# Relative bias loaded as ready rows, and the order of the first loop's loads

## The chip, the cores and the metric

The kernel runs on one core of one Trainium2 chip. Its time is device microseconds of one execution; a lower time is better. Before the change the median of three runs is 983.15 us (982.04 to 983.37).

## The reference, cut to what matters

One decoder block works on 256 tokens of width 1024. A conditioning vector c gives, by one large matrix product, six modulation vectors (shift, scale and gate for the attention half and for the expert half). Then:

```
mod = (silu(c) @ ada_w + ada_b).reshape(6, D_MODEL)
h   = rmsnorm(x, norm1_g) * (1 + sc_a) + sh_a
x   = x + g_a * mixer(h)        # mixer: proj = h @ w_in (1024 x 2840), then attention, then w_out
h   = rmsnorm(x, norm2_g) * (1 + sc_f) + sh_f
x   = x + g_f * peer_ffn(h)     # 16384 experts, top 16 of them for each of 8 heads
out = rmsnorm(x, final_g)
```

The mixer has eight heads of sparse attention in three branches and four heads of differential attention. To the logits of all twelve heads a relative bias is added, `rel_bias[t5_bucket(t - s), head]`: it depends on the distance of query t and key s alone, through 32 buckets. Keys behind the query are masked.

## The kernel before, in words

All tensors lie with 128 partitions. The matrix products of the first half are done in three passes of fp32r: each operand x is split into hi (a cast on ScalarE) and lo (x minus hi, on VectorE), and a product is hi·hi + hi·lo + lo·hi (`mm3`, lines 88 to 91, three matmuls).

The projection loop (lines 246 to 284) goes over the eight slices of 128 rows of the model width, k = 0 to 7. One k-step needs four tiles of 512 KB from memory: two of weights (`w_inK` and `w_inK2`, tile `raw`, a pool of five) and two of modulation weights (`ada_w`, rows of the shift and of the scale, tile `adaw`, four of them). `k_load` (226) issues the four on SP's queue. `k_prep` (230) works on them: VectorE multiplies each modulation tile with the conditioning vector and sums (`ada_sum`, 150; the accumulated value is one column of `mod`); ScalarE casts both weight tiles (lines 73 and 237) and VectorE forms their lo parts (74 and 243); VectorE forms `gs` (239) and the normed slice `t` (241), from which ScalarE makes h_hi (242) and VectorE h_lo (244). `k_mm` (246) then issues 48 matmuls of 128x256 into all eight PSUM banks: 24 with the first weight tile, 24 with the second. The hi and lo parts of the first tile (`w_hi`, `w_lo`) have three buffers, those of the second (`wb`) two. Loads run two steps ahead, `k_prep` one step ahead of the matmuls.

Before the loop, c is loaded and brought to all partitions by two matmuls (262), x is squared and summed (266 to 269), and its root and reciprocal give `rstd1` (270, 271).

The bias comes into being on the chip. A one-hot matrix of the buckets over 384 distances and the table (`buckets`, loaded first on SP after c) are multiplied on TensorE (`bias_sum`, 182), giving one row of 384 values for each head. POOL's queue writes this row 32 times to memory (`fdr`, 180) and reads it back in four transfers of 32 partitions, each partition shifted by one element (`bias_load`, 187), so that `bias[p, head, m]` holds the bias of distance 128 + p - m, with the sign turned. In the program these two stand in step 6; POOL has nothing else to do before them.

From line 129 to 665 the order of instructions is written out by hand, engine by engine (`manual_schedule`). The rest (mixer, expert stage) is ordered by a planner from its own costs, for the mixer after the list `ORDER`; it may put an instruction from behind the loop between two of the loop's on an engine. `lambdas` (193) and the evacuation of the eight banks (661 to 664) close the part ordered by hand. Then come the mixer with its own weights (`w_inA`, `w_inB`, `cmp_w1`, in tiles of the same pool `raw`) and 24 further modulation tiles, from about 78 to 215 us, and the expert stage to the end.

Of the kernel before, what the change touches and what calls it, by code (L numbers as in the profile page):

```python
# [13 lines left out]
F32 = mybir.dt.float32  # L14
# [10 lines left out]
P = 128  # L25
# [17 lines left out]
T = 256  # L43
EPS = 1e-6
NEG = -1e30
# [12 lines left out]
def block_kernel(ctx: ExitStack, tc: tile.TileContext, I, out):  # L58
    nc = tc.nc
    V, S, G, PE = nc.vector, nc.scalar, nc.gpsimd, nc.tensor  # L60
# [4 lines left out]
    dram = ctx.enter_context(tc.tile_pool(name="dram", bufs=1, space=bass.MemoryType.DRAM))  # L65

    def load(src, n=D, pool=None, name="raw", **kw):
        t = (pool or raw_pool).tile([P, D], F32, name=name, **kw)
        nc.sync.dma_start(t[:, :n], src)
        return t  # L70
# [48 lines left out]
    early = early_stack.enter_context(tc.tile_pool(name="early", bufs=1))  # L119

    def bank(tag):
        return (pst if tag == "tr" else psp).tile([P, 512], F32, name=tag)
# [22 lines left out]
    def ada_load(ct):  # L145
        w = early.tile([P, D], F32, name="adaw", bufs=4)
        nc.sync.dma_start(w, I["ada_w"][ct])
        return w

    def ada_sum(ct, w):  # L150
        return V.tensor_tensor_reduce(out=w, in0=w, in1=cond, scale=D / 2, scalar=0.0,
                               op0=ALU.mult, op1=ALU.add, accum_out=mod[:, ct:ct + 1])
# [12 lines left out]
    V.memset(rowmask[0:31], 0.0)  # L165
    nlam = one.tile([P, 1], F32, name="nlam")
    subs = one.tile([P, 1], F32, name="subs")
    hflat = early.tile([P, 1348], F32, name="small")
    buckets = hflat[0:64, 0:396]
    fsb = hflat[0:12, 512:896]  # L170
    lam = hflat[:, 1024:1280].rearrange("p (a b) -> p a b", a=4)
    lj = hflat[:, 1280:1344]
    ls = hflat[:, 1344:1348]
    R = 32
    fdr = dram.tile([12, R, 384], F32, name="fdr")

    def late_loads():
        nc.sync.dma_start(cmpc, I["cmp_small"])
        nc.sync.dma_start(hflat[:, 1024:1280], I["lam"].partition_broadcast(P))
        nc.gpsimd.dma_start(fdr, fsb[:, None, :].to_broadcast([12, R, 384]))  # L180

    def bias_sum():
        fps = bank("tr")
        PE.matmul(fps[:12, :384], buckets[:, 384:396], buckets[:, 0:384], start=True, stop=True)
        S.copy(fsb, fps[:12, :384])

    def bias_load():
        for a in range(P // R):
            nc.gpsimd.dma_start(bias[a * R:(a + 1) * R],
                                bass.AP(tensor=fdr.tensor, offset=fdr.offset + 127 - a * R,  # L190
                                        ap=[[383, R], [384 * R, 12], [1, T]]))

    def lambdas():

# [29 lines left out]
    wts = {}  # L224

    def k_load(k):
        wts[k] = [load(I["w_inK"][k]), load(I["w_inK2"][k])]
        wts[k, "ada"] = [ada_load(k), ada_load(8 + k)]

    def k_prep(k):  # L230
        a, b = wts[k]
        for i in range(2):
            ada_sum(8 * i + k, wts[k, "ada"][i])
        wts[k][0] = split_tile(a)
        hl = [early.tile([P, D], F32R, name=f"wb{l}", bufs=2) for l in range(2)]
        wts[k][1] = hl
        S.copy(hl[0], b)
        V.tensor_add(mod[:, k:k + 9:8], mod[:, k:k + 9:8], ada_b[:, k:k + 9:8])
        V.scalar_tensor_tensor(gs[:, k:k + 1], mod[:, 8 + k:9 + k], 1.0, n1[:, k:k + 1], ALU.add, ALU.mult)
        t = early.tile([P, T], F32, name="nrm", bufs=2)  # L240
        V.scalar_tensor_tensor(t, xT[:, k], gs[:, k:k + 1], rstd1, ALU.mult, ALU.mult)
        S.activation(h1[0][:, k], t, AF.Identity, bias=mod[:, k:k + 1])
        V.tensor_sub(hl[1], b, hl[0].bitcast(F32))
        V.scalar_tensor_tensor(h1[1][:, k], t, mod[:, k:k + 1], h1[0][:, k].bitcast(F32), ALU.add, ALU.subtract)

    def k_mm(k):
        if not pre:
            pre.extend(bank(t) for t in ("mm", "mm", "tr", "tr", "lg", "lg", "o", "o"))
        for i in range(16):
            w, c = (wts[k][0], i * P) if i < 8 else (wts[k][1], (i - 8) * P)  # L250
            c = slice(c, c + P)
            mm3(pre[i // 2][:, (i % 2) * T:(i % 2 + 1) * T], (w[0][:, c], w[1][:, c]), (h1[0][:, k], h1[1][:, k]),
                k == 0 and i % 2 == 0, k == KD - 1 and i % 2 == 1)

    nc.sync.dma_start(buckets, I["buckets"])
    for i in range(2):
        nc.sync.dma_start(xT[:, 4 * i:4 * i + 4], I["x"][:, 4 * i:4 * i + 4])
    k_load(0)
# [6 lines left out]
    for k in (0, 4):  # L265
        S.activation(sq1[:, k:k + 4], xT[:, k:k + 4], AF.Square)
        V.tensor_add(sq1[:, k:k + 2], sq1[:, k:k + 2], sq1[:, k + 2:k + 4])
        V.tensor_add(sq1[:, k], sq1[:, k], sq1[:, k + 1])
        PE.matmul(ss[:, :T], rms_ones, sq1[:, k], start=k == 0, stop=k == 4)
    S.activation(rstd1, ss[:, :T], AF.Sqrt, bias=eps_t)  # L270
    V.reciprocal(rstd1, rstd1)
    bias_sum()
    k_load(1)
    k_prep(0)
    for k in range(KD):
        if k == 6:
            late_loads()
        if k + 2 < KD:
            k_load(k + 2)
        if k + 1 < KD:  # L280
            k_prep(k + 1)
        if k == 6:
            bias_load()
        k_mm(k)
    lambdas()
    early_stack.close()
    wk_stack = ph1.enter_context(ExitStack())
# [938 lines left out]
        outputs(False, None)  # L1226


def bucket_onehot():
    m = np.arange(384)  # L1230
    d = 255 - m
    n = np.maximum(d, 0)
    nf = np.maximum(n, 1).astype(np.float32)
    large = 16 + (np.log(nf / np.float32(16)) / np.float32(math.log(8.0)) * np.float32(16)).astype(np.int32)
    b = np.where(n < 16, n, np.minimum(large, 31))
    o = np.zeros((64, 384), np.float32)
    dd = d >= 0
    o[b[dd], m[dd]] = -1.0
    o[32, ~dd] = -1.0
    return o  # L1240


def layouts(a):
    c = np.ascontiguousarray
    o = {}
    o["x"] = c(a["x"].reshape(T, KD, P).transpose(2, 1, 0))
    o["c"] = c(a["c"].reshape(D))
    table = np.full((64, 12), np.float32(NEG))
    table[:32] = a["rel_bias"]
    o["buckets"] = c(np.concatenate([bucket_onehot(), table], axis=1))  # L1250
    o["ada_w"] = c(a["ada_w"][0].T.reshape(48, P, D))
    o["rows"] = c(np.concatenate([a["norm1_g"].reshape(KD, P).T, a["norm2_g"].reshape(KD, P).T,
                                  a["ada_b"].reshape(48, P).T, a["diff_subln_g"].reshape(P, 1)], axis=1))
    w = a["w_in"][0]
    def colsT(w, c0):
        return w[:, c0:c0 + P].reshape(KD, P, P).transpose(1, 0, 2).reshape(P, D)

    def colsK(cols, w=w):
        return np.concatenate([w[:, c0:c0 + P].reshape(KD, P, P) for c0 in cols], axis=2)

    wq = w.copy()
    wq[:, :512] = w[:, :512].reshape(D, 2, 4, 64).transpose(0, 2, 1, 3).reshape(D, 512)
    start = dict(k0=768, k1=1024, ck=512, cv=640)
    for i in range(4):
        start.update({f"q{i}": P * i, f"dq{i}": 1304 + P * i, f"dk{i}": 1816 + P * i})
    o["w_inK"] = c(colsK([start[n] for n in CHUNKS[:8]], wq))
    o["w_inK2"] = c(colsK([start[n] for n in CHUNKS[8:]], wq))
    wa = np.concatenate([w[:, 896:1024], w[:, 1152:1280], w[:, 1280:1304]], axis=1)
    o["w_inA"] = c(wa.reshape(KD, P, 280).transpose(1, 0, 2).reshape(P, KD * 280))
    o["w_inB"] = c(w[:, 2328:2840].reshape(KD, P, 512).transpose(1, 0, 2).reshape(P, KD * 512))  # L1270
    o["w_out"] = c(a["w_out"][0].reshape(2, 4, P, 4, 256).transpose(3, 0, 2, 1, 4).reshape(4, 2, P, D))
    pos = a["cmp_pos"][0]
    pos = np.concatenate([pos[:, :16].transpose(2, 0, 1), pos[:, 16:].transpose(2, 0, 1)], axis=0)
    w1 = a["cmp_w1"][0].reshape(2, 2, 4, 4, 64, 256)
    o["cmp_w1"] = c(w1.transpose(0, 2, 1, 4, 3, 5).reshape(2, 4, P, D))
    w2 = np.tile(a["cmp_w2"][0].reshape(2, 2, P, 64).transpose(2, 0, 1, 3), (1, 1, 1, 2))
    o["cmp_small"] = c(np.concatenate([pos.reshape(P, 32), w2.reshape(P, 512)], axis=1))
    o["lam"] = c(np.concatenate([a[n].reshape(64) for n in ("lam_q1", "lam_k1", "lam_q2", "lam_k2")]))
    o["peer_wq"] = c(np.stack([colsT(a["peer_wq"][0], i * P) for i in range(16)]))
    o["peer_sub_keys"] = c(a["peer_sub_keys"][0].transpose(2, 0, 1))  # L1280
    o["peer_u"] = c(a["peer_u"][0].reshape(P, P, KD, P).transpose(1, 3, 2, 0).reshape(P, P, D))
    o["peer_v"] = c(a["peer_v"][0].reshape(P, P, D).transpose(1, 0, 2))
    o["final_g"] = c(a["final_g"])
    return o
# [12 lines left out]
```

## Time and profile before

| | |
|---|---|
| profiled execution | 982.88 us |
| its span, first to last instruction | 980.8 us |
| median of three runs | 983.15 us |
| TensorE matmul, weight load busy | 934.2 us (95%), 686.2 us (70%) |
| VectorE, ScalarE, GpSimd busy | 766.8 us (78%), 494.2 us (50%), 17.9 us (2%) |
| read from memory | 193.22 MB |

Times of rows are counted from the span's start. PE is TensorE, PEld its weight loads, DVE VectorE, ACT ScalarE, POOL GpSimd, SP SyncE, which here only issues transfers; a q behind a name (SPq) is the engine's instruction queue. Matmuls overlap each other, so the distance of two starts is what one costs. The granted clock is a share of the full 2.4 GHz.

### The profile page before, as it was taken

To read this page: it belongs to the slowest core of one execution; us is meant where nothing else is said; L and a number is where in the kernel's file an instruction comes from. 1 tells how busy PE (TensorE), PEld (TensorE's weight loads), DVE (VectorE), ACT (ScalarE), POOL (GpSimd) and SP (SyncE) were. 2 spreads that over 40 slices of the span, in tenths; PEclk is the share of its full clock that TensorE was granted. 3 is DMA by queue.
4 is the path that set the end of the run, shared out by engine and by line. 5 is a ranking of instruction groups with operands and counts; after the bars stand their busy time and mean duration, and the time that the engine had idled before them with its cause. 6 is when DMAs were issued, how large, how long until landed. Compare 5 with 4: busy or idle time off the path is not lost.

```text
span 980.8 us, 18690 instructions
## 1 busy us (share of the span) xinstructions
PE 934.2 (95%) x7120; PEld 686.2 (70%) x7120; DVE 766.8 (78%) x2033; ACT 494.2 (50%) x899; POOL 17.9 (2%) x32
## 2 busy tenths in 40 slices
PE   5698997989999999999999999999999999999995
PEld 3697776979888888889999999544444443454442
DVE  6597879778657599658888888799999998656564
ACT  4246876475323365544444444544544554555542
POOL 0100010000000000000000000000000000000001
PEclk9899899899999999999999999999999999999998
DMA  8997646677554345765555555665555669756631
GB/s 285 319 329 252 218 130 211 224 252 263 174 193 151 108 166 179 248 203 177 190 175 191 175 187 179 204 205 193 184 189 188 214 208 332 235 178 207 199 124 48
DMA packets 54709, 198.26 MB, mean 202 GB/s; under 512 B 6269, under 2 KB 6605, under 8 KB 54226
## 3 DMA queue, kind: packets, MB, share of 16 engines
q1 hardware_dynamic: 52642, 189.90, 58.0%
q0 software_dynamic: 1248, 5.33, 2.1%
q10 hardware_dynamic: 720, 1.74, 0.5%
q8 instruction: 58, 0.95, 0.4%
q14 instruction: 41, 0.34, 0.1%
HBM read 193.22 MB, written 3.74 MB: 201 GB/s over the span
## 4 chain that ended last, share of the span: by engine, by line
PE 81%; DVE 7%; DMA 6%; ACT 3%; issue 2%; SPq 0%; DVEq 0%; ACTq 0%
PE y L1089 28%; PE up L89 11%; PE up L91 11%; PE up L90 11%; PE up L877 4%; PE gps L1000 3%; DMA raw<-in_ada_w_dram 3%; DMA adaw<-in_ada_w_dram 2%; PE mm L90 1%; PE mm L91 1%; PE mm L89 1%; PE lg L362 1%; PE o L536 1%; DVE w_lo L74 1%; PE gps L885 1%
## 5 line engine op out<-in xcount | busy, mean ns | idle before, releaser
L1089 PEld LDWEIGHTS <-wt 128*128 128x128 f16 x1500 | 143.9, 98 | 170.2 <-DVE wt L806 4.7
L805 ACT ACTIVATE w_lo<-raw 128x1024 f16<-128x1024 f32 x128 | 135.3, 1057 | 173.9 <-PE y L1089 83.3
L805 ACT ACTIVATE w_hi<-raw 128x1024 f16<-128x1024 f32 x128 | 135.2, 1056 | 170.5 <-PE up L91 85.4
L806 DVE SCALAR_TENSOR_TENSOR w_lo<-raw,w_lo 128x1024 f16<-128x1024 f32 x128 | 156.5, 1222 | 62.9 <-ACT w_lo L805 60.5
L806 DVE SCALAR_TENSOR_TENSOR w_hi<-raw,w_hi 128x1024 f16<-128x1024 f32 x128 | 156.2, 1220 | 54.6 <-ACT w_hi L805 54.4
L1089 PE MATMUL y<-w_hi,wt 128*128 128x512 f16 x756 | 174.0, 379 | 2.1 <-DVE wt L806 2.1
L1089 PE MATMUL y<-w_lo,wt 128*128 128x512 f16 x744 | 171.0, 379 | 0.2
L89 PE MATMUL up<-h,w_hi 128*128 128x256 f16 x512 | 139.6, 273 | 2.1 <-ACT bq L777 2.1
L90 PE MATMUL up<-h,w_hi 128*128 128x256 f16 x512 | 139.6, 273 | 0.0
L91 PE MATMUL up<-h,w_hi 128*128 128x256 f16 x512 | 139.6, 273 | 0.0
L89 PE MATMUL up<-h,w_lo 128*128 128x256 f16 x504 | 137.4, 273 | 0.0
L90 PE MATMUL up<-h,w_lo 128*128 128x256 f16 x504 | 137.4, 273 | 0.0
L91 PE MATMUL up<-h,w_lo 128*128 128x256 f16 x504 | 137.4, 273 | 0.0
L806 DVE SCALAR_TENSOR_TENSOR wt<-st,wt 128x256 f16<-128x256 f32 x128 | 53.7, 420 | 4.7 <-ACT wt L805 4.7
L90 PEld LDWEIGHTS <-w_hi 128*128 128x128 f16 x512 | 50.1, 98 | 8.2 <-issue 2.3
L805 ACT ACTIVATE wt<-st 128x256 f16<-128x256 f32 x128 | 51.3, 401 | 7.6 <-PE y L1089 5.6
L90 PEld LDWEIGHTS <-w_lo 128*128 128x128 f16 x512 | 50.1, 98 | 6.0
L91 PEld LDWEIGHTS <-w_lo 128*128 128x128 f16 x512 | 50.1, 98 | 5.8
L91 PEld LDWEIGHTS <-w_hi 128*128 128x128 f16 x512 | 50.1, 98 | 5.8
L89 PEld LDWEIGHTS <-w_lo 128*128 128x128 f16 x512 | 50.1, 98 | 5.7
L89 PEld LDWEIGHTS <-w_hi 128*128 128x128 f16 x512 | 50.2, 98 | 5.5
L984 DVE TENSOR_TENSOR B<-iota,kT 128x576 f16<-128x576 f16 (+1 forms) x64 | 27.2, 425 | 28.8 <-PE gps L1000 28.8
(370 smaller groups left out, 1505.8 us busy)
## 6 DMA issues: line engine op xcount, KB each, us to landing
raw<-in_peer_u_dram SPq DMA_DIRECT2D x128, 512.0 KB, 3.5
raw<-in_peer_v_dram SPq DMA_DIRECT2D x128, 512.0 KB, 4.2
adal<-in_ada_w_dram SPq DMA_DIRECT2D x24, 512.0 KB, 4.3
raw<-in_w_inK_dram SPq DMA_DIRECT2D x16, 512.0 KB, 8.3
adaw<-in_ada_w_dram SPq DMA_DIRECT2D x16, 512.0 KB, 8.6
wraw<-in_peer_wq_dram SPq DMA_DIRECT2D x12, 512.0 KB, 4.4
raw<-in_cmp_w_dram SPq DMA_DIRECT2D x8, 512.0 KB, 5.0
raw<-in_w_out_dram SPq DMA_DIRECT2D x8, 512.0 KB, 4.3
```

Source lines behind the costliest of these rows:

```text
L74: return (eng or V).tensor_sub(lo, src, hi.bitcast(F32))
L89: PE.matmul(ps, w[0], m[0], start=start, stop=False)
L90: PE.matmul(ps, w[0], m[1], start=False, stop=False)
L91: PE.matmul(ps, w[1], m[0], start=False, stop=stop)
L362: PE.matmul(out, q[x][pr, ts], rhs, start=i == 0, stop=i == 2)
L536: PE.matmul(o[:, h * 64:(h + 1) * 64], pt[:, h * P:(h + 1) * P], vst[sb][:, b, g], start=False, stop=bi == len(blocks) - 1 and h == 3)
L805: S.activation(hi, src, AF.Copy, scale=scale, **kw)
L806: V.scalar_tensor_tensor(lo, src, scale, hi, ALU.mult, ALU.subtract, accum_out=chk[:, i:i + 1])
L877: PE.matmul(ps, w[:, k * P:(k + 1) * P], h2[:, k], start=k == 0, stop=k == KD - 1)
L984: V.tensor_tensor(pairs(x), io, kT[:, i, t0:t0 + NT, None, :].to_broadcast(four), ALU.is_equal)
L1000: PE.matmul(ps[:, q, 0:n], A[:, q], Bg[i][:, q], start=i == 0, stop=i == 1)
L1089: PE.matmul(yps[t][n], w[:, ts], m[:, ns], start=j == 0 and first, stop=j == NJ - 1 and last)
```

## The change

- The host lays out the whole bias, 128 x 12 x 256 values, by indexing the table (`bias_rows`); the kernel loads it in one transfer on SP, in `late_loads`, which stands in step 6, behind the loads of step 7. The matrix of buckets, the matmul, the copy, the write to `fdr` and the four loads from it are gone, with 1024 of the 1348 columns of the tile `small`.
- The sign is turned on the chip: three multiplications by -1 on ScalarE behind the loop's last `k_mm`.
- `k_load` issues the two modulation tiles first, then the two weight tiles.
- `w_inK2` has three tiles of its own (`raw2`, in the pool that closes after the loop); `w_inK` keeps the pool `raw`.
- The modulation sums of step 0 stand ahead of the square root and the reciprocal of the norm.

```diff
-    hflat = early.tile([P, 1348], F32, name="small")
-    buckets = hflat[0:64, 0:396]
-    fsb = hflat[0:12, 512:896]
...
+    hflat = early.tile([P, 324], F32, name="small")
...
     def late_loads():
         nc.sync.dma_start(cmpc, I["cmp_small"])
-        nc.sync.dma_start(hflat[:, 1024:1280], I["lam"].partition_broadcast(P))
-        nc.gpsimd.dma_start(fdr, fsb[:, None, :].to_broadcast([12, R, 384]))
-
-    def bias_sum():
-        fps = bank("tr")
-        PE.matmul(fps[:12, :384], buckets[:, 384:396], buckets[:, 0:384], start=True, stop=True)
-        S.copy(fsb, fps[:12, :384])
-
-    def bias_load():
-        for a in range(P // R):
-            nc.gpsimd.dma_start(bias[a * R:(a + 1) * R],
-                                bass.AP(tensor=fdr.tensor, offset=fdr.offset + 127 - a * R,
-                                        ap=[[383, R], [384 * R, 12], [1, T]]))
+        nc.sync.dma_start(hflat[:, 0:256], I["lam"].partition_broadcast(P))
+        nc.sync.dma_start(bias, I["bias"])
...
     def k_load(k):
-        wts[k] = [load(I["w_inK"][k]), load(I["w_inK2"][k])]
         wts[k, "ada"] = [ada_load(k), ada_load(8 + k)]
+        wts[k] = [load(I["w_inK"][k]), load(I["w_inK2"][k], pool=early, name="raw2", bufs=3)]
+
+    def k_sums(k):
+        for i in range(2):
+            ada_sum(8 * i + k, wts[k, "ada"][i])
 
     def k_prep(k):
         a, b = wts[k]
-        for i in range(2):
-            ada_sum(8 * i + k, wts[k, "ada"][i])
+        if k:
+            k_sums(k)
...
-    nc.sync.dma_start(buckets, I["buckets"])
...
         PE.matmul(ss[:, :T], rms_ones, sq1[:, k], start=k == 0, stop=k == 4)
+    k_sums(0)
     S.activation(rstd1, ss[:, :T], AF.Sqrt, bias=eps_t)
     V.reciprocal(rstd1, rstd1)
-    bias_sum()
...
-        if k == 6:
-            bias_load()
         k_mm(k)
+    for i in range(3):
+        S.mul(bias[:, 4 * i:4 * i + 4], bias[:, 4 * i:4 * i + 4], -1.0)
     lambdas()
```

## Rows read from the trace of the kernel before

**Rows 1.** Waits, 0 to 78 us: waiter, releaser: us in total, times, longest.

```profile
PE mm L89 <- ACT h_hi L242: 13.0, 2, 7.4
...
DVE adaw L151 <- DMA adaw<-in_ada_w_dram: 10.1, 3, 5.6
```

**Rows 2.** TensorE in order of time: start, duration, engine, line, tiles, [idle before, releaser].

```profile
19.46 0.58 PE L90 MATMUL mm<-h_lo,w_hi 128*128 128x256 f32 x1 [0.41 <-DVE h_lo L244]
...
27.09 0.28 PE L89 MATMUL mm<-h_hi,w_hi 128*128 128x256 f32 x1
...
32.79 0.28 PE L89 MATMUL mm<-h_hi,w_hi 128*128 128x256 f32 x1
...
46.23 0.58 PE L89 MATMUL mm<-h_hi,w_hi 128*128 128x256 f32 x1 [7.38 <-ACT h_hi L242]
47.22 0.58 PE L90 MATMUL mm<-h_lo,w_hi 128*128 128x256 f32 x1 [0.41 <-DVE h_lo L244]
...
54.64 0.28 PE L89 MATMUL mm<-h_hi,w_hi 128*128 128x256 f32 x1
...
77.35 0.28 PE L91 MATMUL o<-h_hi,wb 128*128 128x256 f32 x1
```

**Rows 3.** Stretches: busy by engine, then granted clock, DMA share, GB/s.

```profile
20.00:25.00 5.00, 5.00 (x30) 5.00 (x29) 4.93 (x10) 1.54 (x3) 0.23 (x1) 1.00 0.81 162
...
45.00:50.00 5.00, 3.36 (x14) 3.07 (x15) 4.83 (x9) 2.39 (x3) 0.00 (x0) 0.50 1.03 410
```

**Rows 4.** Loads issued at 31, 56 to 58, 2.8 and 3.8 us: last, us to landing.

```profile
adaw<-in_ada_w_dram SPq DMA_DIRECT2D x2, 512.0 KB, 16.6
...
adaw<-in_ada_w_dram SPq DMA_DIRECT2D x2, 512.0 KB, 6.7
...
raw<-in_w_inK_dram SPq DMA_DIRECT2D x2, 512.0 KB, 7.0
...
adaw<-in_ada_w_dram SPq DMA_DIRECT2D x2, 512.0 KB, 8.6
```

**Rows 5.** POOL in order of time.

```profile
13.62 0.88 POOL L180 DMA_DIRECT2D fdr<-small  x1 [12.31 <-ACT small L185]
24.77 2.49 POOL L189 DMA_DIRECT2D bias<-fdr  x4 [10.27 <-DMA fdr<-small]
27.25 0.58 POOL L389 MEMSET vbd<- 128x256 f32 x2
```

**Rows 6.** VectorE in order of time.

```profile
11.97 1.75 DVE L271 RECIPROCAL rstd<-rstd 128x256 f32<-128x256 f32 x1 [1.88 <-ACT rstd L270]
...
13.64 1.16 DVE L151 CUSTOM_DVE_ANT_0 adaw<-adaw,cond 128x1024 f32<-128x1024 f32 x1
...
15.87 1.22 DVE L74 TENSOR_TENSOR w_lo<-raw,w_hi 128x1024 fp32r<-128x1024 f32 x1
...
58.88 1.22 DVE L151 CUSTOM_DVE_ANT_0 adaw<-adaw,cond 128x1024 f32<-128x1024 f32 x1
...
64.64 1.22 DVE L151 CUSTOM_DVE_ANT_0 adaw<-adaw,cond 128x1024 f32<-128x1024 f32 x1
```

**Rows 7.** SP's issues in order of time.

```profile
1.15 0.56 SPq L255 DMA_DIRECT2D small<-in_buckets_dram  x1
...
2.85 0.91 SPq L69 DMA_DIRECT2D raw<-in_w_inK_dram  x2
3.79 1.28 SPq L147 DMA_DIRECT2D adaw<-in_ada_w_dram  x2
```

**Rows 8.** ScalarE in order of time.

```profile
7.84 1.06 ACT L266 ACTIVATE sq<-xT 128x1024 f32<-128x1024 f32 x1 [0.20 <-DMA xT<-in_x_dram]
...
67.75 0.90 ACT L73 CAST w_hi<-raw 128x840 fp32r<-128x840 f32 x1 [0.52 <-DMA raw<-in_w_inA_dram]
...
74.71 0.90 ACT L73 CAST w_hi<-raw 128x840 fp32r<-128x840 f32 x1 [2.78 <-PE tr L90]
...
77.66 0.38 ACT L347 ACTIVATE dq<-mm 128x256 fp32r<-128x256 f32 x1 [2.06 <-PE o L91]
```

More of the change, by code (lines that the diff above doesn't have):

```diff
@@ L167, in block_kernel @@
     subs = one.tile([P, 1], F32, name="subs")
-    hflat = early.tile([P, 1348], F32, name="small")
-    buckets = hflat[0:64, 0:396]
-    fsb = hflat[0:12, 512:896]
[L171 to L175, printed above, removed]
+    hflat = early.tile([P, 324], F32, name="small")
+    lam = hflat[:, 0:256].rearrange("p (a b) -> p a b", a=4)
+    lj = hflat[:, 256:320]
+    ls = hflat[:, 320:324]
     def late_loads():
         nc.sync.dma_start(cmpc, I["cmp_small"])
-        nc.sync.dma_start(hflat[:, 1024:1280], I["lam"].partition_broadcast(P))
-        nc.gpsimd.dma_start(fdr, fsb[:, None, :].to_broadcast([12, R, 384]))
-    def bias_sum():
-        fps = bank("tr")
-        PE.matmul(fps[:12, :384], buckets[:, 384:396], buckets[:, 0:384], start=True, stop=True)
-        S.copy(fsb, fps[:12, :384])
-    def bias_load():
-        for a in range(P // R):
-            nc.gpsimd.dma_start(bias[a * R:(a + 1) * R],
-                                bass.AP(tensor=fdr.tensor, offset=fdr.offset + 127 - a * R,
-                                        ap=[[383, R], [384 * R, 12], [1, T]]))
+        nc.sync.dma_start(hflat[:, 0:256], I["lam"].partition_broadcast(P))
+        nc.sync.dma_start(bias, I["bias"])
     def lambdas():
@@ L1226, in block_kernel, with bias_rows @@
         outputs(False, None)
-def bucket_onehot():
-    m = np.arange(384)
-    d = 255 - m
+def bias_rows(rel_bias):
+    d = 128 + np.arange(P)[:, None] - np.arange(T)[None, :]
     n = np.maximum(d, 0)
@@ L1234, in bucket_onehot @@
     large = 16 + (np.log(nf / np.float32(16)) / np.float32(math.log(8.0)) * np.float32(16)).astype(np.int32)
[L1235 to L1240, printed above, removed]
+    b = np.where(d < 0, 32, np.where(n < 16, n, np.minimum(large, 31)))
+    table = np.concatenate([rel_bias, np.full((1, 12), np.float32(NEG))])
+    return table[b].transpose(0, 2, 1)
 def layouts(a):
@@ L1247, in layouts @@
     o["c"] = c(a["c"].reshape(D))
-    table = np.full((64, 12), np.float32(NEG))
-    table[:32] = a["rel_bias"]
-    o["buckets"] = c(np.concatenate([bucket_onehot(), table], axis=1))
+    o["bias"] = c(bias_rows(a["rel_bias"]))
     o["ada_w"] = c(a["ada_w"][0].T.reshape(48, P, D))
```

## The prediction

> **What bounds the kernel now.** I read the waits of the first 78 us first, then TensorE's matmuls in time, then what the transfers did in the hole that these show. The change touches only the projection loop, which runs eight k-steps from about 18 to 77.5 us; everything behind it (mixer, expert stage) keeps its instructions.
>
> TensorE waited 13.0 us for h_hi in two waits (one is that for the loop's first matmul), and VectorE 10.1 us for adaw, the modulation tiles, in three [rows 1]. The matmuls say what that cost [rows 2]. A k-step is 48 matmuls. The four steps from 54.64 to the last matmul's end (77.35 plus one spacing of 0.12, so 77.47) took 22.83 us, 5.71 each; the step that began at 27.09 took 5.70. Step 2 began at 32.79 and should have ended at 38.49. Step 3 put out one matmul at 46.23 after 7.38 us of idle, its second at 47.22, and ended at 54.64. So steps 2 and 3 took 21.85 us in place of 11.41: 10.4 us lost, of which 8 are waiting and the rest half clock (granted 0.50, which is 1.2 GHz, from 45 to 50, behind the idle) [rows 3].
>
> The hole is a transfer's. From 31 us a pair of adaw tiles took 16.6 us to land; at 56 to 58 us the same pair took 6.7 [rows 4]. In between nothing of the weights had changed. What had gone by then was POOL's traffic: the copy into fdr from 13.62 and four bias transfers from 24.77 on [rows 5]. While the fdr copy ran, 20 to 25 us, the engines were 0.81 busy and moved 162 GB/s; with weights alone, 45 to 50 us, 1.03 and 410 [rows 3]. With 410 GB/s a k-step's four tiles (2.10 MB) need 5.1 us, VectorE's chain for one step 5.76 (58.88 to 64.64) [rows 6], TensorE 5.71. Left alone, the loop is bound by VectorE and TensorE together, not by transfers.
>
> **The change part by part.**
> *POOL's bias path goes* (fdr copy, four bias transfers, one small matmul, one copy on ScalarE). Worth: the 10.4 us of steps 2 and 3, if nothing else is late there. What is late next? Modulation tiles for step k+2 may go out when the sums of step k are done, 11.5 us (two VectorE periods) before the sums that need them start, less 2.3 us for the sums themselves: 9.2 us against a landing of 6.7 undisturbed [rows 4]. The weights follow them on SP's queue and are needed about 1 us later still. Transfers drop out of the way by 2 us or more a step. TensorE then needs step k at start + 5.71 k, VectorE delivers at 5.76 k with the lead that step 0's slow first matmuls give it (step 0 took 7.63 us, from 19.46 to 27.09) [rows 2]: 7.63 against 5.76 is a lead of 1.9 us, less 0.05 for each of seven steps. So the loop ends by TensorE. Bounds of this part: at most 10.4; at least 6.6, if the bias transfer in its new place takes its own 3.8 us (below). I take 10.4, since the undisturbed steps are the nearest rows.
>
> *The start.* adaw(0) now goes out ahead of the weights, and the load of buckets (0.56 us of SP's issue) is gone [rows 7]. Before, the first weight pair went out at 2.85 and landed 7.0 us later, at about 9.9; adaw(0) went out at 3.79 and took 8.6, to 12.4 [rows 4, 7]. Order of issue was order of landing, so the two swap: adaw(0) at about 9.4 to 9.9 and 0.9 later the second tile, weights from about 12. The two sums last 2.23 us (13.64 to 15.87) [rows 6]; they fit between 9.9 and 12.1, where VectorE waited for the norm's square root. The reciprocal began at 11.97 and the next instruction at 13.64; now the first weight subtraction follows it directly, at 13.4 to 13.9 instead of 15.87 [rows 6]. The weights from about 12 on leave time for the cast that this subtraction needs. From there to the second matmul (19.46) the chain is unchanged, 3.6 us, so that matmul comes at 17.0 to 17.5. Bounds: 2.8 gained if xT, too, lands 0.56 us earlier and the sums never hold the reciprocal up; 0.2 if adaw(0) lands only that much earlier than it did: 11.8, the sums to 14.0, the reciprocal's 1.7 to 15.7. I take 2.3, the middle of 17.0 to 17.5, as the order of landing stands in the rows.
>
> *Weights in two pools.* w_inK2 gets three tiles of its own, so w_inK has five alone. SP no longer stands before a full pool; it stands before adaw's four. Nothing is queued behind it there but the same step's weights. Cost 0; with the cover of 2 us a step gone it would be paid once a step.
>
> *The bias on SP.* 128 x 12 x 256 x 4 bytes, 1.57 MB, behind step 7's weights, cmpc and lam. SP gets there when the sums of step 5 are done, about 42 us, and is at the bias at about 45. Step 7's 2.1 MB, 0.4 MB and the 1.57 MB at 410 GB/s [rows 3] put it down at about 53. Behind it on SP wait w_inA's and the compressor's first weights, 3.8 us later than without it; w_inA's first cast stood at 67.75, 9.8 us before the loop's end (in its place now about 55) [rows 8]. So they are just in time, and what they feed starts only after the loop. Price 0, at most 3.8.
>
> *The sign on ScalarE.* Three multiplications of 128 x 1024: like the square at 7.84, 1.06 us each [rows 8], 3.2 us, behind step 7's work and ahead of the lambdas and the evacuations. ScalarE stood idle 2.78 us before the cast at 74.71 and 2.06 before the first evacuation at 77.66 [rows 8], 4.84 in all, for matmuls. That covers 3.2 with 1.6 left. Price 0; 3.2 at most if the cover were gone.
>
> A rule of the Trainium skill speaks against part of this. The rows show that POOL's transfers slowed SP's [rows 4, 5]. "DMA: Bandwidth & Descriptors", section "Issuing engines are not separate DMA queues", says that transfers from any engine end on the same 16 DMA engines and interleave, so that the issuing engine changes hardly anything. By it the 1.57 MB of bias are not saved by their move to SP, only shifted, and the sum would be 12.7 less 3.8, or 8.9, if the transfers have no slack where they now fall; the rows' 5.1 us of transfer in a step of 5.76 say that they have.
>
> **Sum.** 10.4 + 2.3 = 12.7 us. The profiled execution took 982.88 (span 980.8 and 2.1 around it): 970.2. The median of the runs shown is 983.15, 0.27 above it: 970.4. I forecast that the shift passes whole to the end: behind the loop the first idle times are waits on engines, and the loads there go out by free buffers, which move along.
>
> **The rivals.**
> *The bias collides* (0.2). Its 1.57 MB stand before loads that somebody waits for: step 7's tiles while all share the engines, or w_inA's. For it: w_inA's cast was just in time before. Against: 2 us slack, and those weights are used after the evacuations only. 12.7 less 3.8, from 983.15: 974.2.
> *Part is given back in the mixer* (0.1). The order of the instructions behind the loop is set by a planner from its own costs; another start can give it another order, and the layout of the early buffers that the mixer's tiles lie on moves. Against: the engines end the loop in the same distances as before. As a size I take 5 us, half the hole: 975.4.
> *The hole stays* (0.04). It came from SP's queue order and four adaw tiles, not from POOL's traffic; then only the start is gained: 980.8. Against it stand 162 and 410 GB/s.
> *Casts from behind the loop slip into it* (0.06): the slower side. The weight pool has now two free tiles from the second step on; the planner may load w_inA and the compressor's first weights into them and cast them early. They would hold two of the three w_hi tiles until the loop is over. Then the cast for step k+1 waits until TensorE is through the first half of step k (2.85 us), and with the cast (1.06), the subtraction and the rest of VectorE's chain to h_lo (3.6) a step takes 7.5 in place of 5.7: seven steps, 12.6, and the 0.95 MB loaded ahead another 2.3 at the start. 14.9 against the gain of 12.7: 985. It decides when both tiles are taken before step 2. For it: w_inA's cast did stand ahead of step 7's last work [rows 8]. Against: POOL's memsets, which wait for nothing, came only behind the loop's POOL work [rows 5], so the planner does not reach far ahead.
>
> **How the numbers follow.** The forecast has 0.6, with 968 to 972.5 as its own spread (2 us either way for what the planner makes of the mixer). From 967.5 to 976 the range holds it, the collision and most of the mixer's case. A difference under 0.2%, 2 us, cannot be told from none. Faster by more: 0.92 (forecast, collision, mixer, half of the hole that stays); the same 0.03; slower 0.05.
>
> **What would show it.** Right: no transfer on POOL's queue before 78 us; adaw landing in 7 to 9 us throughout; TensorE without a wait of a microsecond between its second matmul of the loop and the last, and its clock full from the fourth microsecond on; the second matmul at about 17.1, the loop's end at 64.8 in place of 77.5; ScalarE's three multiplications done before the first evacuation, at about 65. Wrong: VectorE waiting for adaw or ScalarE for raw in steps 1 to 4; ScalarE standing before the multiplication until the bias lands; casts of w_inA in front of step 6; or a loop that ends at 65 with the expert stage starting less than 11 us earlier.

## The result

The changed kernel took **971.25 us** (median of four runs, 968.78 to 973.18) against 982.6 us (four runs, 981.1 to 983.37) on the same chip: ratio **0.9879**, 95% interval [0.9863, 0.9896]. The forecast was 970.4 with a range of 967.5 to 976.0. The profiled execution is the fastest of the four, 968.78 (span 967.0, where before had 980.8), so its trace flatters the change by some 2 us; the table of the experiments shows a part of why.

The waits from 0 to 65 us, of the kernel after. The 13.0 us for h_hi [rows 1] are down to the one wait of the loop's first matmul, and no VectorE wait for adaw is left.

```profile
PE mm L89 <- ACT h_hi L231: 5.1, 1, 5.1
```

TensorE in order of time: the loop's second matmul, the starts of steps 1 and 4, the loop's last matmul, and the first one behind it.

```profile
17.44 0.58 PE L90 MATMUL mm<-h_lo,w_hi 128*128 128x256 f32 x1 [0.41 <-DVE h_lo L233]
...
24.33 0.28 PE L89 MATMUL mm<-h_hi,w_hi 128*128 128x256 f32 x1
...
41.45 0.28 PE L89 MATMUL mm<-h_hi,w_hi 128*128 128x256 f32 x1
...
64.16 0.28 PE L91 MATMUL o<-h_hi,wb 128*128 128x256 f32 x1
67.44 0.40 PE L89 MATMUL mm<-w_hi,h_hi 128*128 128x280 f32 x1 [3.00 <-DVE q L336]
```

The second matmul came 2.02 us earlier than in [rows 2]. From 24.33 to 41.45 three steps took 17.12, or 5.71 each: the hole is gone. The loop's end moved from 77.47 to 64.28, by 13.2 us. The stretches say why (columns as in [rows 3]):

```profile
20.00:25.00 5.00, 5.00 (x43) 5.00 (x43) 4.93 (x9) 1.99 (x3) 0.00 (x0) 1.00 1.03 410
...
45.00:50.00 5.00, 5.00 (x45) 5.00 (x44) 4.93 (x10) 2.13 (x3) 0.00 (x0) 1.00 1.01 366
...
65.00:70.00 5.00, 2.33 (x10) 2.00 (x10) 4.42 (x9) 2.88 (x6) 0.00 (x0) 0.79 0.90 316
70.00:75.00 5.00, 4.92 (x34) 4.67 (x35) 4.37 (x11) 1.86 (x5) 0.00 (x0) 0.87 1.01 351
```

From 20 to 25 us SP's loads moved 410 GB/s, where 162 were moved while POOL copied [rows 3]. VectorE was busy 4.93 of each 5 us: it and TensorE set the pace. The clock stayed at 1.00 to the loop's end; behind it, it was 0.79 and 0.87.

Loads issued from 30 to 34 us, and the bias (last column: us to landing):

```profile
adaw<-in_ada_w_dram SPq DMA_DIRECT2D x2, 512.0 KB, 4.8
...
bias<-in_bias_dram SPq DMA_DIRECT2D x1, 1536.0 KB, 11.7
```

The adaw pair took 4.8 us in place of 16.6 [rows 4]. ScalarE at the end of the loop, which is the one place where something new is late (compare [rows 8]):

```profile
57.81 2.96 ACT L272 ACTIVATE bias<-bias 128x1024 f32<-128x1024 f32 x3 [1.19 <-DMA bias<-in_bias_dram]
60.78 1.28 ACT L183 ACT_TABLE_LOAD   x1
...
62.19 0.88 ACT L73 CAST w_hi<-raw 128x840 fp32r<-128x840 f32 x1
64.48 0.38 ACT L335 ACTIVATE dq<-mm 128x256 fp32r<-128x256 f32 x1 [1.41 <-PE o L91]
64.76 1.83 ACT L73 CAST w_hi<-raw 128x1024 fp32r<-128x1024 f32 x2
66.48 0.39 ACT L335 ACTIVATE q<-mm 128x256 fp32r<-128x256 f32 x1
```

The bias landed at 57.8, the sign change and the table load held w_inA's cast to 62.19, and two casts stand between the two evacuations that TensorE waits for. It restarted 3.2 us behind the loop's end (64.28 to 67.44); before, 2.0 (77.47 to 79.44):

```profile
79.44 0.39 PE L89 MATMUL mm<-w_hi,h_hi 128*128 128x280 f32 x1 [1.81 <-DVE q L348]
```

### The profile page after: what moved, and what is told of

The parts are those of the page before. It is cut to its first block, busy times and chain, and to the rows that moved or that the text cites. A ratio compares the mean times of both kernels' runs of the same rounds, so it can differ in the third digit from the quotient of the medians.

```text
span 967.0 us, 18674 instructions
## 1 busy us (share of the span) xinstructions
PE 927.8 (96%) x7118; PEld 681.8 (71%) x7118; DVE 765.9 (79%) x2033; ACT 496.2 (51%) x901; POOL 14.5 (2%) x27
## 3 DMA queue, kind: packets, MB, share of 16 engines
q10 hardware_dynamic: 720, 1.74, 0.5%
## 4 chain that ended last, share of the span: by engine, by line
PE 85%; DVE 6%; DMA 4%; ACT 3%; issue 2%; SPq 0%; DVEq 0%; ACTq 0%
PE y L1077 28%; PE up L89 11%; PE up L90 11%; PE up L91 11%; PE up L865 4%; PE gps L988 3%; DMA raw<-in_ada_w_dram 2%; PE lg L350 2%; PE mm L90 1%; PE mm L91 1%; PE mm L89 1%; PE o L524 1%; DMA raw<-in_w_inK_dram 1%; PE gps L873 1%; DVE w_hi L794 1%
```

## The experiments

**The theory** was the prediction's: POOL's bias traffic makes the hole, the early modulation sums bring the start forward, and the rest costs nothing or up to a microsecond at the seam between loop and mixer. The rivals: load order and tile pool make the hole; the copy into fdr makes it and the four reads don't; the sign and the late bias cost time.

One table for all runs, read from the profiles: when the loop's second matmul began, how long step 0 lasted from there, when the loop ended, how long after that TensorE stood still (restart), how long the mixer lasted from the loop's end to the first matmul into `up`, what the clock was short of in the mixer (stretches of some 5 us, each one's length times 1 minus its granted clock, summed), and the measured ratio with its interval.

```
                          2nd   step 0   loop  restart  mixer  clock  ratio to before
before                   19.46   7.63   77.47     2.0   138.9   6.8   1
after                    17.44   6.89   64.28     3.2   137.9   5.1   0.9879 [0.9863, 0.9896]
e1 bias path only        19.31   8.36   67.62     3.2   139.8   8.5   0.9904 [0.9880, 0.9927]
e2 order only            17.81   7.35   74.15     2.0   139.5   6.8   0.9975 [0.9963, 0.9988]
e5 reads late            20.70   7.14   69.13    11.1   146.6  12.0   1.0042 [1.0021, 1.0064]
e6 sums late             19.18   7.83   66.96     3.2   139.5   6.8   0.9899 [0.9876, 0.9922]
e7 bias at the start     18.83   7.36   66.14     2.4   138.8   6.8   0.9893 [0.9870, 0.9917]
e3 sign on GpSimd        17.23   8.26   65.43     3.2   140.6   8.5   0.9917 [0.9904, 0.9930]
e9 same, bias late       17.29   7.17   64.41     2.0   142.0  10.3   0.9886 [0.9871, 0.9900]
e10 sign on VectorE      17.23   8.13   65.30     2.8   140.6   6.8   0.9925 [0.9909, 0.9940]
e12 bias a step earlier  17.40   8.19   65.54     2.0   139.1   6.8   0.9871 [0.9854, 0.9889]
e13 more bytes           17.33   8.32   65.60     3.2   140.0   8.5   0.9866 [0.9851, 0.9882]
e11 sign on a sliver     17.42   7.34   64.71     3.2   142.2  10.3   0.9891 [0.9874, 0.9908]
```

Two things in these profiles go beside the table. In every kernel without a wait in the loop, each of steps 1 to 6 took 5.71 us (e5 is told below), so what differs there is the start and step 0. And the planner wrote TensorE's part of the mixer in one order in after, e1, e6 and e13, in that of before in e2, e3, e7, e9, e11 and e12, and in orders of their own in e5 and e10.

**e1: the bias path alone.** The new bias load and the sign change as in the kernel after; load order, tile pool and sums as before.

```diff
+        wts[k] = [load(I["w_inK"][k]), load(I["w_inK2"][k])]
         wts[k, "ada"] = [ada_load(k), ada_load(8 + k)]
-        wts[k] = [load(I["w_inK"][k]), load(I["w_inK2"][k], pool=early, name="raw2", bufs=3)]
...
-        if k:
-            k_sums(k)
+        k_sums(k)
...
-    k_sums(0)
```

> The kernel before with the bias path of the kernel after alone: rows from memory on SP behind step 7's loads, sign on ScalarE; the order of the loads (weights first), the one pool of five weight tiles and the place of the first sums are those of before. Theory (the hole in steps 2 and 3 is POOL's traffic): the hole goes, the loop's second matmul stays near 19.5 us and the loop ends near 67, so about 972.5 to 974.5. Rival (the hole comes from SP's order and the full pools): VectorE still waits several us for adaw at steps 2 and 3, the loop ends near 75, about 980.

The hole went with POOL's traffic alone: no wait of a microsecond of TensorE's in the loop, end 67.6, 9.9 us earlier than before with a start 0.15 earlier.

**e2: order, pool and early sums alone**: the change's edits to `k_load`, `k_sums` and `k_prep` on the kernel before, with the old bias path.

> The kernel before with its bias path over POOL and memory kept, and the rest of the change: modulation tiles ahead of the weights, w_inK2 in three tiles of its own, the sums of step 0 ahead of the root. Theory (traffic): the start is gained (second matmul near 17.4), but while the copy into fdr and the four reads run, step 2 or 3 waits again, 4 to 10 us; about 976 to 981. Rival (order and pools): no wait over 1 us in the loop, about 971 to 973. Both may hold in part: loads that go out 6 us earlier get more of their bytes down ahead of the copy.

The start moved (17.81), the hole stayed. Three views of this kernel: its waits from 17 to 75 us, TensorE behind the hole, and two stretches.

```profile
ACT w_hi L73 <- DMA raw<-in_w_inK_dram: 17.3, 5, 6.3
```

```profile
41.64 0.38 PE L89 MATMUL mm<-h_hi,w_hi 128*128 128x256 f32 x1 [4.82 <-ACT h_hi L246]
```

```profile
20.00:25.00 5.00, 5.00 (x38) 5.00 (x38) 4.58 (x10) 0.51 (x1) 0.00 (x0) 1.00 0.94 232
30.00:35.00 5.00, 5.00 (x44) 4.97 (x43) 3.20 (x6) 0.00 (x0) 0.00 (x0) 1.00 1.03 238
```

From 30 to 35 us the engines' share was 1.03, yet 238 GB/s were moved, where the kernel after moved 353 to 410 at shares of 1.00 to 1.03: while the four reads of fdr run, the engines are held for longer a byte. The reads go in rows of 1 KB (256 columns of float32, by their access pattern). That the small rows are the reason is argued, not shown. With the modulation tiles first, the wait is ScalarE's for the weights and no longer VectorE's for adaw. The gains of the two halves, 9.1 us of e1's median (973.49) and 2.2 of e2's (980.44) on the 982.61 of before, add up to 11.3; the whole gave 11.4 in its own comparison.

**e5: the four reads late.** The kernel before, its reads of fdr on SP behind step 7's loads, the copy into fdr left where it was.

```diff
-            nc.gpsimd.dma_start(bias[a * R:(a + 1) * R],
+            nc.sync.dma_start(bias[a * R:(a + 1) * R],
```

> The kernel before with the four reads from fdr issued by SP behind the loads of step 7 in place of POOL at 25 us; the copy into fdr stays where it was. It divides the hole between the copy and the reads. Theory (both take transfer time, the copy by its slow 162 GB/s, the reads by their 1.57 MB in 1 KB pieces): TensorE's wait ahead of step 2 or 3 shrinks from 7.4 us to 1 to 4, the loop ends at 70 to 74, the reads stand ahead of the mixer's first weights; 975 to 979. Rival (the copy alone makes the hole): wait as before, 981 to 983. Other rival (the reads alone do): no wait of a microsecond, loop end near 67, 972 to 974.

With the copy alone the loop ended at 69.13, 8.3 us earlier than before though its second matmul began 1.2 later, and no wait of TensorE's in it reached a microsecond. Steps 2 and 3 took 6.43 and 6.15 us in place of 13.44 and 8.41: of the hole's 10.4 us the copy alone leaves 1.2, so the hole needs the reads. Whether the reads would make it without the copy ahead of them is not shown. Issued by SP, the reads were as slow as from POOL: from 55 to 60 and 60 to 65 us, 240 and 200 GB/s at shares of 1.02 and 1.14. So it isn't POOL's queue.

All of the gain was lost behind the loop: the median was 987.81 (982.04 to 993.28, the profile being the fastest), outside of all three forecasts. ScalarE:

```profile
69.33 0.38 ACT L347 ACTIVATE dq<-mm 128x256 fp32r<-128x256 f32 x1 [5.30 <-PE o L91]
...
81.03 0.91 ACT L73 CAST w_hi<-raw 128x840 fp32r<-128x840 f32 x1
```

The cast of w_inA, which stood 10 us ahead of the loop's end [rows 8], came 12 us behind it, and TensorE restarted 11.1 us behind it; the mixer took 146.6 us, the longest of all. w_inA's first tile, issued behind the reads at 55.50, landed 13.6 us later, at 69.1, so the cast at 81.03 waited for the planner's other order too; the two parts are not told apart. Here the rival "given back in the mixer" is real, in a kernel that is not the change.

**e6: step 0's sums where they were**, behind the square root.

```diff
-        if k:
-            k_sums(k)
+        k_sums(k)
...
-    k_sums(0)
     S.activation(rstd1, ss[:, :T], AF.Sqrt, bias=eps_t)
```

> The kernel after with the sums of step 0 back behind the reciprocal; nothing else. Theory: the reciprocal comes at 12.0 in place of 12.25, the sums behind it, so the loop's second matmul comes 2.0 us later than in the kernel after (19.4 in place of 17.44) and the whole 1.5 to 2.2 us later, about 973. Rival (the start is set by the weights' landing, not by the sums' place): the matmul stays within 0.5 us and so does the time.

The second matmul came at 19.18, 1.74 later than after; that is what the early sums are worth in the loop. The median rose by 1.7 us too, inside the interval. The loop's end came 2.7 us later, as step 0 lasted 7.83 us in place of 6.89.

**e7: the bias at the start**, on POOL's queue in place of SP's.

```diff
-        nc.sync.dma_start(bias, I["bias"])
+        nc.gpsimd.dma_start(bias, I["bias"])
```

> The kernel after with the bias transfer issued by POOL, which is free from 1 us on, so that its 1.57 MB go out beside the loads of x and of step 0; the sign stays on ScalarE behind the loop. Theory (all transfers share the same engines, and at the start there is no slack): x, adaw(0) and the weights of step 0 land up to 3.8 us later, the loop's second matmul comes near 20 to 21 in place of 17.44, but ScalarE no longer waits 1.2 us for the bias and the mixer's first weights land 3.8 us earlier; about 972 to 974.5. Rival (a transfer of this size has room anywhere in the first 60 us): 969.5 to 971.

Issued at 1.30 us it landed 9.4 later and pushed step 0's loads back: second matmul 18.83, 1.4 later than after, where 3 was expected; loop end 66.1. It had landed before the loop began, so it doesn't show what such a load does beside the loop. It does show that POOL's queue as such isn't slow: from 5 to 10 us 386 GB/s at a share of 0.97.

**e3, e9 and e10: the sign off ScalarE.** e3 does the three multiplications on GpSimd, e9 too and issues the bias behind the compressor's first weights, e10 does them on VectorE. In turn:

```diff
-    for i in range(3):
-        S.mul(bias[:, 4 * i:4 * i + 4], bias[:, 4 * i:4 * i + 4], -1.0)
...
         G.memset(z, 0.0)
+    for i in (2, 0, 1):
+        G.tensor_scalar_mul(bias[:, 4 * i:4 * i + 4], bias[:, 4 * i:4 * i + 4], -1.0)
```

```diff
-        nc.sync.dma_start(bias, I["bias"])
...
-    for i in range(3):
-        S.mul(bias[:, 4 * i:4 * i + 4], bias[:, 4 * i:4 * i + 4], -1.0)
...
+            if n == "cmp" and not bias_in:
+                bias_in.append(1)
+                with tc.issue_after(last_load[0]):
+                    nc.sync.dma_start(bias, I["bias"])
+                for i in (2, 0, 1):
+                    G.tensor_scalar_mul(bias[:, 4 * i:4 * i + 4], bias[:, 4 * i:4 * i + 4], -1.0)
```

```diff
-        S.mul(bias[:, 4 * i:4 * i + 4], bias[:, 4 * i:4 * i + 4], -1.0)
+        V.tensor_scalar_mul(bias[:, 4 * i:4 * i + 4], bias[:, 4 * i:4 * i + 4], -1.0)
```

> The kernel after with the three multiplications by -1 on GpSimd, behind its memsets, in place of ScalarE. Theory (the sign and its wait on ScalarE push the mixer's first casts between the evacuations): the casts of w_inA and of the compressor's weights run before the loop ends, the second evacuation follows the first within 0.9 us, TensorE starts again 1.8 us behind the loop's end in place of 3.0; 1.2 us and what the clock then keeps, about 969.5 to 970.2. Rival (the casts wait for weights that land at 59 to 60 us anyway, or GpSimd's long multiplications slow VectorE beside them): restart still 2.5 to 3 us behind, 971 or more.

> As with the sign on GpSimd, and the bias transfer issued behind the mixer's first two weight tiles in place of ahead of them. Theory: those tiles land 3.8 us earlier, at 54 to 56 us, so their casts are done long before the loop ends; restart 1.8 us behind the loop's end, and the mixer's next weights are not later than now; about 969 to 970, no worse than the sign on GpSimd alone. Rival: the bias, or the weights behind it, now come late for the first logits: a wait for the bias on VectorE near 80 us, 971 or more.

> The kernel after with the sign on VectorE, which stands idle from 57.9 to 62.3 us. Theory: three multiplications of at most 1.2 us fit there, ScalarE casts the mixer's first weights from 59 us on, TensorE starts again about 1.8 to 2.2 us behind the loop's end; 969.8 to 970.5. Rival: VectorE's queue then holds up the lambdas and the lo parts of those casts, so that the restart comes no earlier than 3.0 us behind the end: 971 or more.

None was faster than the change, and e3 and e10 were slower, their intervals above its own. e3 restarted no sooner than the change, about as its rival had it. e9 did restart 2.0 us behind the loop's end, and VectorE never waited for the bias, but its median was 972.47: the theory's mechanism with the rival's time. e10 restarted 2.8 behind, between its two cases. In e3 GpSimd took 8.45 us and VectorE beside it was slowed: h_lo's row took 1.26 us where the same row takes 0.48 in the kernel after (at 57.13).

```profile
56.70 8.45 POOL L377 TENSOR_SCALAR bias<-bias 128x1024 f32<-128x1024 f32 x3 [54.43 <-DMA bias<-in_bias_dram]
```

```profile
56.93 1.26 DVE L233 SCALAR_TENSOR_TENSOR h_lo<-nrm,mod,h_hi 128x256 fp32r<-128x256 f32 x1
```

In e10 VectorE took 1.89 us for the three:

```profile
57.32 1.89 DVE L272 TENSOR_SCALAR bias<-bias 128x1024 f32<-128x1024 f32 x3
```

Its span was 6.1 us above that of the kernel after: 1.0 at the loop's end (step 0 lasted 8.13 us in place of 6.89), 2.7 in the mixer (1.7 of it clock), 1.7 in the stage of `up` (403.0 from its first matmul to the next stage's, against 401.3, and that stage lacked 1.7 us of clock against 0.0), 0.7 behind it. So most of the difference is clock and the slow matmuls of step 0. Taking the sign off ScalarE gained nothing; why e3 and e10 are slower in the median is not shown.

**e12, e13, e11: is the seam paid for?** e12 issues the bias ahead of step 7's loads. e13 loads 1.05 MB of it once more, ahead of it, into a tile that is free. e11 multiplies 8 of 256 columns only and leaves the sign of the others unturned.

```diff
+        if k == 5:
+            nc.sync.dma_start(bias, I["bias"])
```

> The changed kernel with one edit: the bias is issued one k-step earlier, ahead of step 7's loads. Theory (transfers have slack in the loop, and what the change gave back is the seam: bias down at 57.8 us, then the sign, then two casts between the two evacuations): step 7's tiles land up to 3.8 us later and nobody waits a microsecond for them; the loop still ends at 64.2 to 64.5; bias down by about 50 us, sign and the casts of the mixer's first weights done before the loop ends, the two evacuations back to back, TensorE restarting about 2 us behind the loop's end in place of 3.2; time 0 to 1.5 us below the changed kernel, ratio to before 0.9865 to 0.988. Rival (the bias collides wherever it stands in front of tiles that are waited for): step 7 waits 2 to 4 us, loop end 66 to 68, ratio 0.990 to 0.992. Rival (the mixer's length goes by where TensorE's half-clock spells fall, not by the seam): seam as clean as in the theory, but the time within 1 us of the changed kernel or above it.

```diff
+        nc.sync.dma_start(sq1, I["bias"][:, 0:8])
         nc.sync.dma_start(bias, I["bias"])
```

> The changed kernel with one addition: 1.05 MB of the bias are loaded once more, into a tile that is no longer needed, ahead of the bias itself; the output is unchanged. Theory (the seam's price comes from the bias and the mixer's first weights landing late): bias down about 2.5 us later, at 60 to 61, the sign to 63.5, w_inA's cast at 65, first evacuation up to 2.5 us later than in the changed kernel; TensorE restarts 4.5 to 6 us behind the loop's end; loop end unchanged at 64.2 to 64.5; time 1.5 to 3 us above the changed kernel, ratio 0.9895 to 0.991. Rival (the price is the sign's ScalarE time only, and transfers have slack here too): restart as in the changed kernel, ratio 0.987 to 0.989.

```diff
-        S.mul(bias[:, 4 * i:4 * i + 4], bias[:, 4 * i:4 * i + 4], -1.0)
+        S.mul(bias[:, 4 * i:4 * i + 4, 0:8], bias[:, 4 * i:4 * i + 4, 0:8], -1.0)
```

> The changed kernel with the sign change done on 8 of 256 columns of each head only (the rest of the bias keeps the wrong sign), so that ScalarE's three multiplications shrink from 3.1 us to well under 1. Theory (the sign's time is part of what the seam gives back): the mixer's first casts stand 2 us earlier and the evacuations are not held up, TensorE restarts 2 to 2.5 us behind the loop's end, time 0 to 1.5 us below the changed kernel, ratio 0.9865 to 0.988. Rival (the sign costs nothing, since its place lies under the loop's last matmuls and the mixer's length is set by the weights and by half-clock spells): within 0.5 us of the changed kernel or above it, ratio 0.9875 to 0.990.

In e12 the seam is clean, as expected: the sign at 56.97, three casts done before the loop's end, the evacuations back to back.

```profile
56.97 2.94 ACT L273 ACTIVATE bias<-bias 128x1024 f32<-128x1024 f32 x3
...
61.33 2.62 ACT L73 CAST w_hi<-raw 128x840 fp32r<-128x840 f32 x3
65.74 0.39 ACT L336 ACTIVATE dq<-mm 128x256 fp32r<-128x256 f32 x1 [1.78 <-PE o L91]
66.61 0.38 ACT L336 ACTIVATE q<-mm 128x256 fp32r<-128x256 f32 x1 [0.49 <-DVE dq L337]
```

TensorE restarted 2.0 us behind the end (65.54 to 67.51), as in the kernel before, and the 1.57 MB ahead of step 7's tiles made TensorE wait for nothing. The ratio was 0.9871 against 0.9879. That lies inside the theory's range (0.9865 to 0.988), and the median, 971.81, within the third case's microsecond of the change: the two are not told apart, as the difference looked for, 1.2 us, is smaller than either interval. In e13 the sign waited longer for the bias:

```profile
58.89 2.95 ACT L273 ACTIVATE bias<-bias 128x1024 f32<-128x1024 f32 x3 [2.38 <-DMA bias<-in_bias_dram]
```

That is 1.1 us later, not the 2.5 I expected. The loop ended 1.3 us later too, so TensorE restarted 3.2 us behind the loop's end, exactly as in the kernel after: e13 did not lengthen the seam, and its ratio of 0.9866 says nothing of what a longer one would cost. e11 shortened the sign to 0.47 us and restarted 3.2 us behind the end as well. There ScalarE stood idle for 4.9 us ahead of the first evacuation, and a cast still stood between the two, though its tile had landed at 59.5. So it is the place of the casts that makes the restart late, more than the sign. The ratio, 0.9891, lies in its rival's range.

What the seam costs the profiles can say a little better, over the table's thirteen rows. The mixer lasted 131 to 135 us plus the clock it was short of. Among the kernels with the order of before, this rest is 131.8 to 132.7 us where the restart took 2.0 us, and 132.0 and 132.1 where it took 3.2 (e11 and e3). So apart from the clock the later restart isn't seen. The clock may be its price: in all six profiles that restarted 3.2 us behind the loop's end, a stretch of half clock begins within 5.4 us of that end; of the six that restarted 2.0 to 2.8 behind, only e9's has one there. But the others lose clock later in the mixer, 6.8 us in all against 5.1 to 10.3, so no sum of the two shows.

What tells the profiles apart is the clock. e13 and the kernel after have the same instructions in the same order on TensorE, ScalarE, VectorE and GpSimd; e13 only issues one more load. e11 has the other order. The mixer as one stretch, after, e13 and e11 in turn:

```profile
64.28:202.16 137.88, 123.43 (x801) 104.45 (x800) 116.46 (x326) 98.51 (x277) 6.81 (x10) 0.96 0.68 223
```

```profile
65.36:205.56 140.20, 125.96 (x802) 106.62 (x801) 116.34 (x326) 98.86 (x276) 6.80 (x10) 0.94 0.65 218
```

```profile
64.47:206.92 142.45, 127.38 (x802) 107.49 (x801) 116.40 (x326) 98.94 (x277) 6.87 (x10) 0.93 0.65 219
```

(The last two stretches begin 0.24 us ahead of their loops' ends.) VectorE's work is 116.3 to 116.5 in all three; TensorE's busy time goes from 123.4 to 127.4, as the granted clock goes from 0.96 to 0.93. Behind the waits of the seam and of the mixer the clock falls for a stretch, and the profiled execution of the kernel after has the shortest such loss of the thirteen. That this differs from one execution of a kernel to the next is seen in the four of the kernel after: the mean granted clock was 0.990 in the fastest, the profiled one, and 0.985 in the slowest (973.18).

## Why the prediction was right

**POOL's bias path, 10.4 us.** Right in cause (e1 and e2 undo it in both directions) and in size: by the trace of after, steps 1 to 7 took 39.95 us (24.33 to 64.28), 5.71 each; the same seven took 50.38 before. The 162 GB/s that the prediction put against 410 were the copy's, from 20 to 25 us, and e5, where the copy is as slow (122 GB/s), shows that it is nearly covered. The stretch that mattered was not read: the four reads ran from 24.77 to about 44 us, and there the kernel before moved 248 GB/s at a full share of the engines. Copy and reads went together, so the sum did not suffer.

```profile
30.00:35.00 5.00, 5.00 (x43) 4.88 (x42) 2.87 (x6) 2.35 (x3) 0.00 (x0) 1.00 1.04 248
```

**The start, 2.3 us.** Measured 2.02, the second matmul at 17.44 in the forecast 17.0 to 17.5; the sums ran from 9.96, the reciprocal at 12.25, the first weight subtraction at 13.91, where 13.4 to 13.9 was said. e6 puts 1.74 of it on the early sums. A further 0.74 came unasked: step 0 took 6.89 in place of 7.63. Its matmuls came 0.21 us apart until 20.16, in place of 23.85 before; in e12 and e13, with the same start, they did so until 23.1 and 23.3, and the loop ended 1.3 us later. The kernel after has the shortest step 0 of all thirteen profiles (6.89 to 8.36), so that gain is luck and not the change's. The granted clock reads 1.00 there because the traces' record of it begins only where the spacing falls to 0.12, at 20.14 in after and 23.78 before.

**Two pools, 0.** No engine waited for a modulation tile behind the start, and the adaw pairs landed in 4.7 to 8.8 us, mostly below the 7 to 9 forecast.

**The bias on SP, price 0.** No wait of TensorE's in the loop came of it, but the landing was wrong: 57.8 in place of 53. With it came one of the marks that the prediction itself had called wrong: ScalarE stood 1.19 us before the multiplication until the bias landed. I let each load land in the order of issue at 410 GB/s. From the bias's issue at 46.1 to 57.8 the engines moved 4.4 MB, at 374 GB/s: 1.8 of what had been issued ahead of it, the bias (1.57), and 1.0 of the mixer's first tiles, which were issued behind it and went down beside it. Order of issue was order of landing for the tiles of one size in [rows 4]; a 1.57-MB load shares the engines with what follows.

**The sign, price 0.** Three multiplications took 2.96, as sized. The cover was counted for the place in the old order; with the bias at 57.8 it was gone, and the restart came 1.2 us later than in the kernel before. e11 shows that this would have come without the sign's time as well, through the place of the casts. That it costs nothing is not shown: e12, which takes the 1.2 us away, cannot tell it from nothing, and e13 left the seam as long as it was.

**The sum.** The loop's end moved by 13.2 where 12.7 was said, and the profiled execution by 14.1. The medians moved by 11.4: the profile of after lies 2.5 below its median of 971.25, the one of before (982.88) 0.3 above the 982.6 of this comparison. The loop's 13.2 holds the 0.74 of step 0, and the clock in the mixer explains a share of the rest: the profiled execution was granted 0.990 and the slowest 0.985, worth 4.8 us of a span of 967 by our estimate, and their spans differ by 4.4. The prediction passed the loop's gain whole to the end; in the medians 1.3 us of its 12.7 did not arrive, and no run shows where they went (the later restart would fit in size). That the median still came within a microsecond of 970.4 is in part luck: the kernel before was 0.55 us faster in this comparison than the 983.15 that the forecast was counted from.

**The rivals.** The bias collides: not seen, in e12 not even ahead of step 7's loads; nor did the sum fall to the 8.9 us that the prediction worked out for a bias that is only shifted. Part is given back in the mixer: its condition came true, as the planner gave TensorE another order there than before, but not its price of 5 us; from loop end to `up` 137.9 against 138.9, and less the clock it lacked 132.8 against 132.1. The hole stays: e1 excludes it. Casts slip into the loop: the first foreign weight cast stood at 62.19.

## What to carry to other kernels

Transfers in small rows can starve large loads beside them, from whichever queue they come: compare GB/s at equal engine share, not the share, read that in the very stretch where the late load was under way, and take the traffic away whole rather than reorder around it. Read a gain at the end of the stage that changed (here 13.2 us at the loop's end), and then ask of what lies behind only whether it still lasts as long; differences of 2 us there came with the clock, in kernels with one and the same order on TensorE. One profile is one execution: here it was the lucky one, in step 0 and in the mixer. A transfer moved out of one stage needs a place where no first load of the next stage stands behind it: e5 won most of the same loop and lost it all, in part that way.

## What the runs showed of the hardware

Engines at 1.03 share moved 238 GB/s with rows of 1 KB among the load (e2), and 353 to 410 without (after); issued by SP in place of POOL, the same reads moved 200 to 240 (e5). A load of 1.57 MB from SP shared the engines with loads issued after it: 1.0 MB of those had moved when it landed. The same 128x1024 multiplication by a constant took 0.99 us on ScalarE (2.96 for three), 0.63 on VectorE and 2.8 on GpSimd, and beside GpSimd's VectorE's h_lo row took 1.26 us in place of 0.48. Matmuls came 0.21 us apart, the spacing from 47.2 us on in before at a granted 0.50, for 2.7 to 6.1 us from the loop's second matmul on, over the thirteen profiles; the granted clock reads 1.00 there only because its record begins behind that.
